# Twelve seven-product pairs in place of ten in the right half of an MLP's down-projection, at other places, and four additions moved from GpSimd to VectorE

## The chip, the cores and the metric

The kernel runs on one core of one Trainium2 chip. A core has TensorE (matrix products; the profile calls it PE, its weight loads PEld), VectorE (DVE), ScalarE (ACT), GpSimd (POOL) and SyncE (SP, which here only issues DMAs). The metric is the device time of one execution in microseconds, the median of the runs shown. The engines run side by side; each works through its own instructions in a fixed order and waits where an operand is not ready or a buffer is not free yet.

## The reference

Two decoder layers over 256 tokens of width 2048, in float32. Each layer has a mixer (attention and a short convolution, with projections in and out) and an MLP of width 8192; both add to x.

```python
for l in range(DEPTH):                       # DEPTH = 2
    h = _rmsnorm(x, attn_norm_g[l])
    proj = h @ w_in[l]                       # q, k, v, gates, convolution input
    ...
    x = x + jnp.concatenate([attn, conv], axis=-1) @ w_out[l]
    hm = _rmsnorm(x, mlp_norm_g[l]) @ w_up[l]               # (256, 2048) @ (2048, 8192)
    x = x + jnp.square(jax.nn.relu(hm)) @ w_down[l]         # (256, 8192) @ (8192, 2048)
```

The change is in the last line: the product with `w_down`, 8192 rows by 2048 columns a layer.

## The kernel before, in words

**Products.** Each float32 operand is split into a high and a low part that TensorE multiplies at its fast rate, and a product is three matmuls: high x high, high x low, low x high (`TERMS`). ScalarE makes a high part by copying (for a weight `whi`, L291), VectorE the low one by subtracting (`wlo`, L292).

**The MLP.** The 8192 hidden rows are worked off as 32 pairs of 128-row blocks, pair 0 to 31, in two passes.

- *First pass:* for each pair the up-projection (`up_part`, `upc` at L855), its squared ReLU (`square`), and, two pairs behind it (`LAG`), the left 1024 columns of the down-projection (`product`, `pr` at L903). At its end pairs 30 and 31 are left, whose left half has a loop of its own (L985, 48 matmuls in all, with weights `draw` and the activations f in two halves). The layer's sums for the left columns are then put together (`shared`, `onto`, and the loop ahead of `store`).
- *Second pass:* the right 1024 columns, pair 0 to 31, products named `rt`. The activations are read back from DRAM.

**Plain and seven-product pairs.** A 2x2 block product can be done with eight block products or with seven products of sums of blocks. A plain pair is eight products (24 matmuls, L1057; the last one at L1042). Its activations come ready split as `g`, a block for two pairs, loaded over GpSimd's queue. A seven-product pair is seven (21 matmuls, L903), but its operands have to be made. `quarters` makes the weights' from the pair's `raw`: b1 and b2 (ScalarE's b1h, b2h at L739, VectorE's b1l, b2l at L740); the sums t in three VectorE operations (L753, L756, L757); from t the parts t13h and t24h (ScalarE) and t13l and t24l (VectorE). `in_forms` makes the activations': h is read back by SyncE (`load_again`, h<-hid), four small VectorE operations (L889 to L892) add the sums, ScalarE copies f's high part (L894), and VectorE subtracts f's low part (L895). In the first pass every pair but the last two is a seven-product pair. In the second, those in `SEVEN` are.

**What sets the order.** TensorE's order is that of the code. For weights, `Weights.take` lets each be made three jobs ahead of its use (`AHEAD = 3`), in an order of jobs that the second pass lays out so: the plain pairs' half-pairs in sequence, and behind each of the four half-pairs ahead of a seven-product pair one of its four jobs (b1 and b2; t and t13; f; t24). Where the seven-product pair before stands only two pairs away, there is one plain pair between them, so two jobs go behind each of its two half-pairs:

```python
for i in SEVEN:
    before = [j for j in mine if j < where[i]][-4:]
    js = [where[i] + k for k in (1, 2, 0, 3)]
    if len(before) == 4 and SEVEN.index(i) and where[SEVEN[SEVEN.index(i) - 1]] > before[0]:
        before = [before[2], before[2], before[3], before[3]]
```

On the other engines a scheduler then fixes the order when the kernel is built. Buffers hold the work back further: three for the `raw` loads of a layer's MLP, three each for a weight's high and low part, two for b1, two for f, one each for b2, t13, t24, t and h. A buffer is written anew only once its readers are done, so a `whi` on ScalarE may wait for TensorE, and a load on SyncE for ScalarE and VectorE.

**Sums and the next norm.** `shared` (L964) forms e1 to e4 from the seven products' sums by `onto` (L961) and adds them to x. It is called once for the left half, ahead of the loop at L985, and once for the right half, behind the last seven-product pair. At the end of layer 0 the next layer's norm transposes x chunk by chunk (`norm.chunk`, `tpn` at L425) as background work between matmuls; `work.start(piece, wait)` puts it off by so many ticks, that is by groups of matmuls. At the end of layer 1 `store` writes the output over SyncE.

## Time and profile before

| | us |
|---|---|
| median of three runs | 2179.25 (2176.77 to 2180.44) |
| the profiled execution, its own time | 2180.75 |
| its span in the trace | 2178.7 |
| TensorE busy | 2151.5 (99%) |
| VectorE busy | 1690.1 (78%) |
| ScalarE busy | 1291.5 (59%) |
| GpSimd busy | 179.3 (8%) |

Three stages recur below. The end of the first pass (L985) lies at 910.57 to 928.21 in layer 0 and at 1990.66 to 2007.04 in layer 1; the second pass at 928.21 to 1098.05 and at 2007.04 to 2174.32. The rows of a timeline give the start in us, the duration, the engine, the line, and out<-in; `x4` behind a row is four instructions put together, and a bracket at the end is the time that the engine waited before it, with what ended the wait. A row of the view by windows gives a stretch, its length, then the busy time of TensorE, its weight loads, VectorE, ScalarE and GpSimd with the number of instructions, the granted clock of TensorE (1.00 is full speed), the busy share of the DMA engines and the GB/s. An engine's busy time says little here by itself: what counts is who is late for TensorE, and where.

### The profile page before, as it was taken

The numbers are of one execution on the slowest core, as the hardware profiler recorded it, in microseconds if no ns is written. First come the engines' busy times: TensorE is split into PE (matmuls) and PEld (weight loads), VectorE is DVE, ScalarE is ACT, GpSimd is POOL, SyncE is SP. The second block draws the span as 40 slices with busy tenths as digits, with TensorE's granted clock in tenths as the row PEclk, the third lists the DMA queues.
The fourth block names the chain that finished last, engine by engine and source line by source line (L and its number), as shares of the span: only waits on it lengthen the run. The fifth ranks groups of instructions, "written<-read, shape, count | busy, mean of one in ns | idle before, by whom it ended". The sixth has DMA issues, their size and how long they took to land.

```text
span 2178.7 us, 29219 instructions
## 1 busy us (share of the span) xinstructions
PE 2151.5 (99%) x11026; PEld 1824.4 (84%) x11026; DVE 1690.1 (78%) x2405; ACT 1291.5 (59%) x1748; POOL 179.3 (8%) x224
## 2 busy tenths in 40 slices
PE   8999999999999999999999999999999999999999
PEld 7888888888888888788878888888888888887887
DVE  5677655698888888898766776556988888888885
ACT  6456444566666666555554554455666666665553
POOL 3011100000000000200100211000000000002001
PEclk9999999999999999999999999999999999999999
DMA  7655766487777777877756566665777777768884
GB/s 254 175 156 174 220 185 189 149 254 219 230 228 218 228 223 230 262 263 266 268 147 182 155 191 206 185 187 180 237 235 224 222 223 226 230 215 275 289 288 137
DMA packets 286013, 469.71 MB, mean 216 GB/s; under 512 B 10579, under 2 KB 191397, under 8 KB 283056
## 3 DMA queue, kind: packets, MB, share of 16 engines
q1 hardware_dynamic: 267552, 412.13, 61.2%
q0 software_dynamic: 18272, 55.70, 7.5%
q8 instruction: 86, 1.41, 0.3%
q14 instruction: 55, 0.45, 0.1%
q10 hardware_dynamic: 48, 0.02, 0.0%
HBM read 437.37 MB, written 30.43 MB: 215 GB/s over the span
## 4 chain that ended last, share of the span: by engine, by line
PE 93%; DVE 2%; DMA 2%; issue 2%; ACT 1%; POOL 0%; ACTq 0%; POOLq 0%; DVEq 0%
PE upc L855 29%; PE pr L903 12%; PE rt L1057 10%; PE o L361 8%; PE rt L903 4%; PE gc L383 4%; PE ci L383 4%; PE gb L383 4%; PE v L361 4%; PE k L361 4%; PE q L361 3%; PE upw L855 1%; DMA uraw<-in_w_up_dram 1%; PE sc L525 1%; PE pr L985 1%
## 5 line engine op out<-in xcount | busy, mean ns | idle before, releaser
L292 DVE TENSOR_TENSOR wlo<-raw,whi 128x1024 fp32r<-128x1024 f32 (+1 forms) x346 | 426.9, 1235 | 272.8 <-ACT whi L291 268.1
L291 ACT ACTIVATE whi<-raw 128x1024 fp32r<-128x1024 f32 (+1 forms) x346 | 363.7, 1054 | 418.4 <-PE o L361 71.9
L855 PE MATMUL upc<-nT,uhi 128*128 128x512 f32 x1920 | 477.6, 391 | 0.0
L718 ACT ACTIVATE uhi<-uraw 128x1024 fp32r<-128x1024 f32 x256 | 271.2, 1060 | 290.2 <-PE upc L855 254.0
L855 PEld LDWEIGHTS upc<-nT,uhi 128*128 128x128 f32 x1920 | 352.7, 188 | 68.3
L719 DVE TENSOR_TENSOR ulo<-uraw,uhi 128x1024 fp32r<-128x1024 f32 x256 | 312.5, 1221 | 116.9 <-ACT uhi L718 110.8
L855 PEld LDWEIGHTS upc<-nT,ulo 128*128 128x128 f32 x1920 | 261.9, 190 | 18.7
L855 PE MATMUL upc<-nT,ulo 128*128 128x256 f32 x1920 | 267.7, 282 | 0.0
L1057 PE MATMUL rt<-whi,g 128*128 128x512 f32 x672 | 210.9, 389 | 0.0
L361 PE MATMUL o<-whi,cat 128*128 128x512 f32 x512 | 159.6, 390 | 0.0
L1057 PEld LDWEIGHTS rt<-whi,g 128*128 128x128 f32 x672 | 126.2, 188 | 26.1
L1057 PE MATMUL rt<-wlo,g 128*128 128x512 f32 x336 | 130.7, 389 | 0.0
L361 PEld LDWEIGHTS o<-whi,cat 128*128 128x128 f32 x512 | 96.2, 188 | 19.7
L895 DVE TENSOR_TENSOR f<-h,f 128x1024 fp32r<-128x1024 f32 (+1 forms) x84 | 102.3, 1218 | 0.0
L882 POOL DMA_DIRECT2D plain<-f x44 | 31.5, 715 | 832.7 <-DVE f L895 786.1
L361 PE MATMUL o<-wlo,cat 128*128 128x512 f32 x256 | 99.7, 389 | 0.0
L740 DVE TENSOR_TENSOR t13l<-t,t13h 128x1024 fp32r<-128x1024 f32 x80 | 97.9, 1223 | 1.9 <-ACT t13h L739 0.5
L740 DVE TENSOR_TENSOR t24l<-t,t24h 128x1024 fp32r<-128x1024 f32 x80 | 97.4, 1217 | 0.6 <-ACT t24h L739 0.3
L903 PE MATMUL pr<-t13h,f 128*128 128x512 f32 x240 | 93.8, 391 | 0.0
L894 ACT ACTIVATE f<-h 128x1024 fp32r<-128x1024 f32 (+1 forms) x84 | 86.1, 1025 | 4.7 <-DVE h L892 4.5
L361 PE MATMUL q<-whi,nT 128*128 128x512 f32 x256 | 85.4, 401 | 3.4 <-ACT whi L291 3.4
L739 ACT ACTIVATE t24h<-t 128x1024 fp32r<-128x1024 f32 x80 | 84.0, 1050 | 4.7 <-PE rt L903 3.0
(365 smaller groups left out, 3898.6 us busy)
## 6 DMA issues: line engine op xcount, KB each, us to landing
uraw<-in_w_up_dram SPq DMA_DIRECT2D x128, 1024.0 KB, 6.6
raw<-in_w_in_dram SPq DMA_DIRECT2D x191, 512.0 KB, 4.0
draw<-in_w_down_dram SPq DMA_DIRECT2D x64, 1024.0 KB, 5.2
raw<-in_w_down_dram SPq DMA_DIRECT2D x64, 1024.0 KB, 6.4
raw<-in_w_out_dram SPq DMA_DIRECT2D x64, 512.0 KB, 3.7
plain<-f POOLq DMA_DIRECT2D x44, 512.0 KB, 6.5
g<-plain POOLq DMA_DIRECT2D x22, 1024.0 KB, 6.3
hid<-h POOLq DMA_DIRECT2D x20, 256.0 KB, 6.2
```

Source lines behind the costliest of these rows:

```text
L291: a = nc.scalar.activation(hi[:, k], raw[:, k], AF.Copy)
L292: d = nc.vector.tensor_sub(lo[:, k], raw[:, k], hi[:, k].bitcast(F32))
L361: nc.tensor.matmul(acc[:, t], a.ap[:, pa, k % KG, t * P:(t + 1) * P], (hi, lo)[pw][:, j], start=(k == 0 and n == 0), stop=(k == nk - 1 and ...
L383: nc.tensor.matmul(acc[:, f, 0] if part else acc[:, f], wt[:, k % 4, fs], a.ap[:, 0, k % KG] if part else a.ap[:, :, k % KG], start=(part ...
L718: nc.scalar.activation(hi, src, AF.Copy)
L719: nc.vector.tensor_sub(lo, src, hi.bitcast(F32))
L740: keep(nc.vector.tensor_sub(lo, src, hi.bitcast(F32)))
L855: nc.tensor.matmul(acc[:, 0] if part else acc, wt[:, k], a.ap[:, 0, k % KG] if part else a.ap[:, :, k % KG], start=(part == 0 and kh == 0 ...
L894: nc.scalar.activation(f[:, 0, :n], h[:, :n], AF.Copy)
L895: nc.vector.tensor_sub(f[:, 1, :n], h[:, :n], f[:, 0, :n].bitcast(F32))
L903: nc.tensor.matmul(prods[n], f[:, pa, a], b[pw], start=(start and m == 0), stop=(stop and m == 2))
L1057: nc.tensor.matmul(prods[p], blocks[b][:, slot, pa, 2 * k + t], w[pw][:, n], start=(i == PLAIN[0] and k == 0 and m == 0), stop=False)
```

## The change

The pairs that use seven products in the second pass are twelve in place of ten, the first is pair 4 in place of 2, and from pair 7 to 25 they stand two apart in place of mostly three; the others are plain. The four additions of `shared` leave GpSimd: the function returns them, and VectorE does them, for the left half behind the `onto`s of the last two pairs, for the right half at once. The transposes of the next layer's last chunk are put off by 8 ticks in place of 2.

```diff
-SEVEN = (2, 5, 8, 11, 14, 16, 19, 22, 25, 27)
+SEVEN = (4, 7, 9, 11, 13, 15, 17, 19, 21, 23, 25, 28)
@@ shared
-                for dst, v in ((x11, e1), (x12, e4), (x21, e3), (x22, e3)):
-                    nc.gpsimd.tensor_tensor(dst, dst, v, op=ALU.add)
+                return [(x11, e1), (x12, e4), (x21, e3), (x22, e3)]
@@ ahead of the first pass's last two pairs
-            shared(*left)
+            sums = shared(*left)
@@ behind them
             for dst, (_, _, p) in zip(left, OWN):
                 onto(dst, prods[p], dst)
+            for dst, v in sums:
+                nc.vector.tensor_add(dst, dst, v)
@@ behind the last seven-product pair
-                        shared(*right)
+                        for dst, v in shared(*right):
+                            nc.vector.tensor_add(dst, dst, v)
@@ behind the last plain pair
-                                work.start(norm.chunk(2 + n, 2))
+                                work.start(norm.chunk(2 + n, 2 + 6 * n))
```

The diff leaves open what the scheduler makes of it. In the rows that follow, the numbers behind names tell buffers' contents apart, and lines of the changed kernel from 970 on are up to two off from those of before.

At the end of layer 1's first pass, VectorE has had these instructions from the last `onto`s of `shared` on (`f<-h,f 128x512` is the low part of pair 31's activations, `wlo<-draw` a weight of the last two pairs, `wlo<-raw` those of the second pass's first plain pairs):

```order
L961 SCALAR_TENSOR_TENSOR e_18283<-pr_13924,rowf_13666,e_18282 128x512
L874 TENSOR_TENSOR h<-h,ratiob 128x2x128
L961 SCALAR_TENSOR_TENSOR e_18285<-pr_13927,rowf_13666,e_18283 128x512
L961 SCALAR_TENSOR_TENSOR x_84<-pr_13927,rowf_13666,x_84 128x512
L961 SCALAR_TENSOR_TENSOR e_18284<-pr_13928,rowf_13666,e_18283 128x512
L740 TENSOR_TENSOR t24l<-t,t24h 128x1024
L292 TENSOR_TENSOR wlo<-draw,whi 128x1024
L895 TENSOR_TENSOR f<-h,f 128x512
L292 TENSOR_TENSOR wlo<-raw,whi 128x1024 x2
```

In the changed kernel the same place on VectorE reads:

```order
L961 SCALAR_TENSOR_TENSOR e_18319<-pr_13960,rowf_13702,e_18318 128x512
L874 TENSOR_TENSOR h<-h,ratiob 128x2x128
L961 SCALAR_TENSOR_TENSOR e_18321<-pr_13963,rowf_13702,e_18319 128x512
L961 SCALAR_TENSOR_TENSOR x_84<-pr_13963,rowf_13702,x_84 128x512
L961 SCALAR_TENSOR_TENSOR e_18320<-pr_13964,rowf_13702,e_18319 128x512
L895 TENSOR_TENSOR f<-h,f 128x512
L292 TENSOR_TENSOR wlo<-draw,whi 128x1024
L292 TENSOR_TENSOR wlo<-raw,whi 128x1024 x2
```

The t24l of the second pass's first seven-product pair has left this place, and f stands ahead of the wlo. The additions of the left half come further down, among the first weights of the second pass.

In the second pass, VectorE of the kernel before has these instructions up to the activations of pair 16, which stands two behind pair 14 (f_19018 is pair 16's, raw_18823 its weights, wlo_18861 and wlo_18895 belong to the plain pairs 15 and 17):

```order
L740 TENSOR_TENSOR b1l_18826<-raw_18823,b1h_18825 128x512
L756 TENSOR_TENSOR t_18872<-t_18872,raw_18823 128x512
L890 TENSOR_TENSOR h_18905<-h_18905 128x128
L292 TENSOR_TENSOR wlo_18861<-raw_18817,whi_18860 128x1024
L757 TENSOR_TENSOR t_18872<-raw_18823,t_18872 128x512
L892 TENSOR_TENSOR h_18905<-h_18905 128x128
L292 TENSOR_TENSOR wlo_18895<-raw_18892,whi_18894 128x1024
L740 TENSOR_TENSOR b2l_18830<-raw_18823,b2h_18829 128x1024
L740 TENSOR_TENSOR t13l_18875<-t_18872,t13h_18874 128x1024
L740 TENSOR_TENSOR t24l_18924<-t_18872,t24h_18923 128x1024
L895 TENSOR_TENSOR f_19018<-h_18905,f_19018 128x1024
```

Here f follows work for its own pair and one weight of the plain pair behind it. In the changed kernel VectorE has these up to the activations of pair 17 (f_19106; t_19158 and raw_19133 are pair 19's, raw_19115 is pair 18's, raw_19201 pair 20's):

```order
L740 TENSOR_TENSOR t13l_19073<-t_19070,t13h_19072 128x1024
L740 TENSOR_TENSOR t24l_19112<-t_19070,t24h_19111 128x1024
L889 TENSOR_TENSOR h_19021<-h_19021 128x128
L891 TENSOR_TENSOR h_19021<-h_19021 128x128
L753 TENSOR_TENSOR t_19158<-raw_19133 128x1024
L890 TENSOR_TENSOR h_19021<-h_19021 128x128
L292 TENSOR_TENSOR wlo_19173<-raw_19115,whi_19172 128x1024
L756 TENSOR_TENSOR t_19158<-t_19158,raw_19133 128x512
L892 TENSOR_TENSOR h_19021<-h_19021 128x128
L292 TENSOR_TENSOR wlo_19204<-raw_19201,whi_19203 128x1024
L757 TENSOR_TENSOR t_19158<-raw_19133,t_19158 128x512
L895 TENSOR_TENSOR f_19106<-h_19021,f_19106 128x1024
```

Now two operations on pair 19's sums and the first weight of pair 20 stand ahead of pair 17's f. On ScalarE the same holds: the last rows up to pair 17's f (f_19018 is pair 15's f) are

```order
L894 ACTIVATE f_19018<-h_18935 128x1024
L291 ACTIVATE whi_19117<-raw_19115 128x1024
L739 ACTIVATE b2h_19051<-raw_19045 128x1024
L739 ACTIVATE b1h_19135<-raw_19133 128x512
L739 ACTIVATE t13h_19072<-t_19070 128x1024
L739 ACTIVATE t24h_19111<-t_19070 128x1024
L291 ACTIVATE whi_19172<-raw_19115 128x1024
L291 ACTIVATE whi_19203<-raw_19201 128x1024
L894 ACTIVATE f_19106<-h_19021 128x1024
```

Both weights of pair 18 and the first of pair 20 are made between the f of pair 15 and the f of pair 17.

## Prediction

> **What bounds the kernel now.** I read the page first, then the stretches, the timelines of TensorE and VectorE, and the groups of the weight loads. The two stretches of some 17 us are the last two pairs of the first pass (layer 0, layer 1); the two long ones are the second pass.
>
> ```profile
> PE 2151.5 (99%) x11026; PEld 1824.4 (84%) x11026; DVE 1690.1 (78%) x2405; ACT 1291.5 (59%) x1748; POOL 179.3 (8%) x224
> ...
> 910.57:928.21 17.64, 14.04 (x49) 11.03 (x48) 12.96 (x13) 6.15 (x8) 8.20 (x5) 0.81 0.74 276
> 1990.66:2007.04 16.38, 12.79 (x49) 10.06 (x48) 12.77 (x13) 6.15 (x8) 8.20 (x5) 0.90 0.80 291
> 928.21:1098.05 169.84, 169.44 (x756) 140.09 (x754) 138.99 (x174) 95.14 (x111) 12.56 (x13) 1.00 0.75 259
> 2007.04:2174.32 167.28, 167.28 (x739) 138.33 (x737) 134.22 (x165) 87.00 (x89) 9.84 (x11) 1.00 0.71 244
> ```
>
> TensorE is the bound: in layer 1's second pass it is busy all the time, 167.28 us for 738 matmuls, 0.227 us each. So a plain pair (24 matmuls) lasts 5.45 us and a seven-product pair (21) 4.77. VectorE is busy for 134 of those 167 us, not far behind. TensorE does lose time at the end of the first pass: 48 matmuls take 17.64 and 16.38 us where 48 x 0.227 = 10.90, and the granted clock (last but two column) is 0.81 and 0.90.
>
> ```profile
> 1996.32 0.39 PE L985 MATMUL pr<-wlo,f 128*128 128x512 f32 x1
> 2000.30 0.73 PE L985 MATMUL pr<-whi,f 128*128 128x512 f32 x2 [3.59 <-DVE f L895]
> ...
> 1993.98 5.72 POOL L972 TENSOR_TENSOR x<-x,e 128x512 f32<-128x512 f32 x3 [1.03 <-DVE e L961]
> ...
> 1994.48 0.73 DVE L961 SCALAR_TENSOR_TENSOR e<-pr,rowf,e 128x512 f32<-128x512 f32 x1
> 1995.14 1.22 DVE L740 TENSOR_TENSOR t24l<-t,t24h 128x1024 fp32r<-128x1024 f32 x1
> 1996.29 2.30 DVE L292 TENSOR_TENSOR wlo<-draw,whi 128x1024 fp32r<-128x1024 f32 x1
> 1998.51 1.74 DVE L895 TENSOR_TENSOR f<-h,f 128x512 fp32r<-128x512 f32 x1
> 2000.17 1.21 DVE L292 TENSOR_TENSOR wlo<-raw,whi 128x1024 fp32r<-128x1024 f32 x1
> ...
> 2006.13 2.72 DVE L961 SCALAR_TENSOR_TENSOR x<-pr,rowf,x 128x512 f32<-128x512 f32 x4
> ```
>
> There TensorE waits 3.59 us for f of pair 31. Ahead of it VectorE has t24l of the first seven-product pair (1.15 us to the next start) and a wlo that takes 2.30 beside GpSimd's adds, as f takes 1.74; the next wlo, after the adds, takes 1.21.
>
> **The change, part by part.** *End of the first pass.* In the new order f(31) stands right behind the last e. Without t24l, wlo and GpSimd's adds it starts about when t24l starts now, 1995.14, and is done within 0.7 us, by 1995.9; TensorE wants its low part two matmuls past 1996.55. The next want, the last wlo, comes one job later, by 1997.1, for 1999.3. So both stretches shrink to 10.90: 6.74 + 5.48 = 12.2 us gained, half-clock time included.
>
> *Matmuls.* Two more seven-product pairs a layer, three matmuls fewer each: 12 x 0.227 = 2.7 us gained.
>
> *Transposes of the last chunk (wait 2 + 6n).* They stand behind 48 matmuls of the next layer's q in place of 12.
>
> ```profile
> 1101.68 0.60 PE L425 MATMUL tpn<-ident,x 128*128 128x128 f32 x4
> 1104.85 0.63 PE L425 MATMUL tpn<-ident,x 128*128 128x128 f32 x4 [2.57 <-DVE nT L256]
> ```
>
> Its 2.57 us wait goes, as 36 more matmuls (8.2 us) cover the release; 24 matmuls (5.4 us) remain before their result is asked for, against 0 now. Gain 2.6 us; bounds 0 and 2.6.
>
> *The second pass* decides. Rows of VectorE, ScalarE and TensorE around pairs 14 and 16, the one place of this trace before pair 25 where seven-product pairs stand two apart:
>
> ```profile
> 2072.20 1.22 DVE L895 TENSOR_TENSOR f<-h,f 128x1024 fp32r<-128x1024 f32 x1
> ...
> 2077.33 1.23 DVE L753 TENSOR_TENSOR t<-raw 128x1024 f32<-128x1024 f32 x1 [2.43 <-DMA raw<-in_w_down_dram]
> ...
> 2079.61 0.28 DVE L889 TENSOR_TENSOR h<-h 128x128 f32<-128x128 f32 x1
> 2079.81 0.28 DVE L891 TENSOR_TENSOR h<-h 128x128 f32<-128x128 f32 x1
> 2080.01 0.69 DVE L740 TENSOR_TENSOR b1l<-raw,b1h 128x512 fp32r<-128x512 f32 x1
> 2080.62 0.69 DVE L756 TENSOR_TENSOR t<-t,raw 128x512 f32<-128x512 f32 x1
> ...
> 2085.63 1.22 DVE L740 TENSOR_TENSOR t13l<-t,t13h 128x1024 fp32r<-128x1024 f32 x1
> 2086.77 1.22 DVE L740 TENSOR_TENSOR t24l<-t,t24h 128x1024 fp32r<-128x1024 f32 x1
> 2087.90 1.22 DVE L895 TENSOR_TENSOR f<-h,f 128x1024 fp32r<-128x1024 f32 x1
> ...
> 2098.51 1.22 DVE L895 TENSOR_TENSOR f<-h,f 128x1024 fp32r<-128x1024 f32 x1
> ...
> 2075.29 1.06 ACT L291 ACTIVATE whi<-raw 128x1024 fp32r<-128x1024 f32 x1 [1.65 <-PE rt L1057]
> ...
> 2085.44 1.06 ACT L739 ACTIVATE t24h<-t 128x1024 fp32r<-128x1024 f32 x1 [0.30 <-PE rt L903]
> 2086.41 1.04 ACT L894 ACTIVATE f<-h 128x1024 fp32r<-128x1024 f32 x1
> ...
> 2085.24 0.39 PE L1057 MATMUL rt<-whi,g 128*128 128x512 f32 x1
> ...
> 2090.68 0.39 PE L903 MATMUL rt<-b1h,f 128*128 128x512 f32 x1
> ...
> DMA to landing us min/median/max: 4.9/6.4/8.1
> ...
> raw<-in_w_down_dram SPq DMA_DIRECT2D x64, 1024.0 KB, 6.4
> ...
> g<-plain POOLq DMA_DIRECT2D x22, 1024.0 KB, 6.3
> hid<-h POOLq DMA_DIRECT2D x20, 256.0 KB, 6.2
> ```
>
> From these: VectorE starts an operation of 1024 elements every 1.14 us, of 512 every 0.60, of 128 every 0.20; ScalarE one of 1024 every 0.97 (done after 1.06). A tile that TensorE frees at a pair's end (2085.24) is written 0.20 later. f of pair 16 was ready at 2089.1, TensorE wanted it at 2090.68: 1.6 us to spare, where pair 14 (f at 2073.4, wanted at 2080.5) had 7.1. The last four rows are the time of a weight load in that pass and the sizes: 1 MB of weights a pair, half a MB of g for each of 44 plain pairs, a quarter for a seven-product pair.
>
> *The sums.* Four adds of 512 elements, 0.60 us each, join VectorE at both ends. At the left they lie ahead of the weights of pairs 1 and 2; priced in the walk below. At the right they lie beside pairs 29 to 31 (16 us, five VectorE weights): nothing. GpSimd only loses work. Layer 1's stores wait for the sums, and pair 3's load stands behind the stores on SyncE; its buffer comes free later still (7.9 us into the pass), so that costs nothing.
>
> VectorE's work for a seven-product pair is 4 x 1.14 (t, b2l, t13l, t24l) + 3 x 0.60 + 4 x 0.20 + 1.14 (f) = 8.30, for a plain pair 2.28. Two apart, that is 10.58 us while TensorE needs 4.77 + 5.45 = 10.22. The new pattern has nine such steps in a row, 7 to 25. By throughput alone 0.36 x 9 = 3 us would be lost at most, and the lead would swallow it. The queues' order does more.
>
> Pair 17: VectorE has wlo of pair 20's first half ahead of f(17), and ScalarE the whi of that half ahead of f(17). That whi reuses a buffer that TensorE frees at the end of pair 16. So even with all else early, f(17)'s low part is ready 0.20 + 1.06 + 0.04 (handing over) + 1.14 (wlo) + 0.60 (t) + 1.22 + 0.04 = 4.30 us after pair 16 ends, and TensorE, which wants it for its third matmul, 0.45 in, waits 3.85. Pair 15: t24l(15) and f(15) stand behind wlo of pair 16's second half, which needs a buffer freed 2.72 into pair 14: 2.72 + 0.20 + 1.06 + 0.04 + 1.14 + 1.14 + 1.22 + 0.04 = 7.56 after pair 13, wanted at 5.45 + 0.45 = 5.90: 1.66. These 5.5 us a layer are the floor.
>
> Loads add to it: a seven-product pair's load goes out when the plain pair three buffers back has been read. I walked the three queues row by row from the start of the pass (0.0), every row starting when its engine is free and what it waits for is done, with a load of 6.4. Where VectorE reaches wlo(2) only behind the sums and pair 4's t, b1l and b2l, at 10.7, it is done 0.9 after TensorE's want. Low part of f, ready/wanted: pair 7 27.3/38.8; 9 42.0/49.0; 11 57.3/59.2; 13 72.1/69.4; 15 84.9/82.3; 17 102.1/95.1 (pair 20's load goes out at 91.6, when b2l(17) is done, and lands at 98.0); 19 109.2/112.4; then t24l(21) 0.9 late, f(23) 0.7, f(25) 4.4. The steps of 15 us from 7 to 13 hold VectorE's waits for loads (the 2.43 above is one such). Sum 19.2 us a layer. With a load of 5.3, nearer the fastest: 0.9 at pair 2, 0.3 at 13, 1.9 at 15, 5.1 at 17, 2.7 at 25, sum 10.9. I take the middle, 15.0: the pass before mostly moves 4.25 MB in three pairs' 15.7 us, the new one 2.75 in two pairs' 10.2 and some 1.5 of waits, 14% less in a us, so loads should land a little faster than the median.
>
> *The clock.* What a wait of TensorE does to it:
>
> ```profile
> 413.96 1.30 PE L855 MATMUL up<-nT,uhi 128*128 128x512 f32 x3 [2.09 <-ACT ev L865]
> ...
> 411.00:414.39 3.39, 1.30 (x10) 1.05 (x9) 0.94 (x1) 1.54 (x2) 0.00 (x0) 1.00 1.01 367
> 414.39:417.81 3.42, 3.42 (x11) 2.77 (x10) 0.62 (x2) 0.32 (x1) 0.00 (x0) 0.50 0.23 80
> ```
>
> A 2.09 us wait that left TensorE busy for 1.30 of 3.39 us was followed by 3.42 us at half clock. The first pass's ends, waits of 3.6, cost beyond the wait (16.38 - 10.90 - 3.75) 1.7 and, in layer 0, 3.0. I take 2.3 a layer for pair 17 and 0.9 for the smaller waits: bounds 1.7 and 4.6.
>
> The Trainium skill ("TensorE: Matmul & The Clock Gate", HAM oscillation) puts the bar at idle gaps over about 3.4 us. The trace disagrees: 2.09 sufficed. By the page, the floor's waits, broken by two matmuls that need only f's high part, would cost no clock; the sum would be 2 x 0.9 lower.
>
> *Sum*, on the profiled execution's 2180.75: - 12.2 - 2.7 - 2.6 + 2 x (15.0 + 3.2) = + 18.9, so 2199.6; that execution was 1.5 over the median of the three runs, so 2198. The case's own range: 2 x (10.9 + 2.3) = 26.4 gives 2188, 2 x (19.2 + 4.6) = 47.6 gives 2209.
>
> **The rivals.** *Faster.* Loads land before they are asked for, only pairs 15 and 17 wait, and those waits don't halve the clock: 2180.75 - 17.5 + 2 x 5.5 - 1.5 = 2173. For it: pairs 16 to 19 now, where f follows f after 10.6 us (2087.90, 2098.51) with no load waited for. Against: 2072.20 to 2087.90, 15.7 us in the one step of the new kind. It decides below 6.5 us of waits a layer. The skill's rule on the clock above would speak for it.
>
> *No change.* The same floor with 2.3 us of half clock a layer: 2177.
>
> *Much slower.* Every step of two takes 15.7 as from 14 to 16: nine steps x (15.7 - 10.2) = 49.5, less the 11.4 that pair 7 has to spare, 38 a layer: 2238. The 10.6 step speaks against it.
>
> *The first pass's end doesn't shorten*, because another row takes f(31)'s place: 12.2 more than forecast, 2210. For it only that the new order is untested there; the walk has 1.1 to spare (1995.9 against 1997.0).
>
> **How the numbers follow.** Forecast 0.68, faster 0.13, no change 0.12, much slower 0.04, first pass unchanged 0.03. What a measurement can tell from no change is about 0.2%, 4.4 us. So faster 0.13, same 0.12, slower 0.75. The range 2176 to 2213 takes in the floor with the clock, the forecast with the slowest loads and the case without the first pass's gain; it leaves out 0.17.
>
> **What would show it.** Right: no wait of L985 on f, and both stretches near 11 us at clock 1.00; GpSimd without additions; in the second pass waits of TensorE for f at pairs 13, 15, 17 and 25, the longest at 17, a clock below 1.00 there, VectorE waiting for raw between; the second pass some 15 us longer than its 166. Wrong: TensorE without waits from pair 7 to 13 and at 25 (loads faster than 5.3), or waits at every pair. Most of all I could be wrong in how far the loads lag.

## The result and the profile after

The changed kernel takes 2195.58 us, the median of four runs (2192.67 to 2198.82), against 2179.32 before: a ratio of 1.0075 (95% interval 1.0063 to 1.0088), 16 us slower. The forecast was 2198.

The page of the changed kernel, its busy times and the chain that ended last; behind them the chain of the kernel before:

```profile
PE 2154.1 (98%) x11014; PEld 1821.4 (83%) x11014; DVE 1716.4 (78%) x2461; ACT 1299.7 (59%) x1760; POOL 148.7 (7%) x206
...
PE 82%; DVE 7%; DMA 7%; issue 2%; ACT 1%; POOL 0%; ACTq 0%; POOLq 0%; DVEq 0%; SPq 0%
```

```profile
PE 93%; DVE 2%; DMA 2%; issue 2%; ACT 1%; POOL 0%; ACTq 0%; POOLq 0%; DVEq 0%
```

TensorE has 12 matmuls fewer and is as busy as before in us, but 11 hundredths of the span have left it in the chain, to VectorE and the DMAs. The same stretches as those shown of before (end of the first pass in layer 0 and 1, second pass in layer 0 and 1):

```profile
906.54:917.42 10.88, 10.88 (x50) 9.01 (x48) 7.54 (x10) 5.18 (x7) 0.71 (x1) 1.00 0.96 343
1995.96:2006.84 10.88, 10.88 (x49) 9.01 (x48) 7.54 (x10) 5.18 (x7) 0.71 (x1) 1.00 0.98 346
917.41:1106.78 189.37, 175.52 (x749) 141.61 (x748) 161.61 (x210) 103.01 (x121) 4.99 (x8) 0.96 0.69 235
2006.84:2192.74 185.90, 172.36 (x733) 139.07 (x731) 157.75 (x201) 94.47 (x99) 3.19 (x6) 0.97 0.64 222
```

The account of the profiled execution, whose span grew by 18.3 (2178.7 to 2197.0):

| stage | before | after | change |
|---|---|---|---|
| layer 0 up to the end of its first pass | 910.57 | 906.54 | -4.0 |
| end of the first pass, layer 0 | 17.64 | 10.88 | -6.8 |
| second pass, layer 0 | 169.84 | 189.37 | +19.5 |
| layer 1 up to the end of its first pass | 892.61 | 889.18 | -3.4 |
| end of the first pass, layer 1 | 16.38 | 10.88 | -5.5 |
| second pass, layer 1, and what follows it | 171.66 | 190.16 | +18.5 |

So the first pass's ends gave 12.3 where 12.2 was forecast, and the second passes took 38. What TensorE waited for in them, first in layer 0, then in layer 1, by the view of waits (us in total, times, longest):

```profile
PE rt L903 <- ACT f L894: 9.7, 4, 6.5
PE rt L903 <- DVE f L895: 3.1, 4, 1.0
PE rt L1059 <- DVE wlo L292: 0.7, 1, 0.7
PE rt L1044 <- DVE x L961: 0.3, 1, 0.3
...
PE rt L903 <- ACT f L894: 8.7, 4, 5.1
PE rt L903 <- DVE f L895: 4.2, 4, 2.0
PE rt L1059 <- DVE wlo L292: 0.7, 1, 0.7
```

These are 13.8 and 13.5 us a layer. From the starts of the pairs' first matmuls, the time that a pair and the start of the next one lost against 5.44 (plain) or 4.76 (seven products), half clock included:

| lost at | layer 0 | layer 1 | forecast, without the clock (loads of 5.3 to 6.4 us) |
|---|---|---|---|
| pair 2 | 1.0 | 1.0 | 0.9 |
| pairs 12 and 13 | 2.9 | 2.9 | 0.3 to 2.7 |
| pairs 14 and 15 | 2.0 | 1.9 | 1.9 to 2.6 |
| pairs 16 and 17 | 10.9 | 8.3 | 5.1 to 7.0 |
| pairs 20 to 23 | 0 | 0 | 0 to 1.6 |
| pairs 24 and 25 | 4.1 | 5.7 | 2.7 to 4.4 |

Over the whole pass that is 20.9 us in layer 0 and 20.0 in layer 1. In layer 0 the 2.5 us are left out that its last four pairs lose before the change too, beside the next layer's transposes; all losses of a second pass below are counted so.

The longest wait is that of pair 17. VectorE and ScalarE ahead of it, in layer 0, and TensorE:

```profile
1006.12 1.22 DVE L740 TENSOR_TENSOR b2l<-raw,b2h 128x1024 fp32r<-128x1024 f32 x1
1010.38 0.69 DVE L740 TENSOR_TENSOR b1l<-raw,b1h 128x512 fp32r<-128x512 f32 x1 [3.04 <-ACT b1h L739]
...
1015.15 0.28 DVE L890 TENSOR_TENSOR h<-h 128x128 f32<-128x128 f32 x1
1015.35 1.22 DVE L292 TENSOR_TENSOR wlo<-raw,whi 128x1024 fp32r<-128x1024 f32 x1
1016.48 0.68 DVE L756 TENSOR_TENSOR t<-t,raw 128x512 f32<-128x512 f32 x1
1017.09 0.28 DVE L892 TENSOR_TENSOR h<-h 128x128 f32<-128x128 f32 x1
...
1009.71 0.63 ACT L739 ACTIVATE b1h<-raw 128x512 fp32r<-128x512 f32 x1 [4.73 <-DMA raw<-in_w_down_dram]
...
1017.40 1.06 ACT L894 ACTIVATE f<-h 128x1024 fp32r<-128x1024 f32 x1 [2.10 <-DVE h L892]
...
1018.51 0.79 PE L903 MATMUL rt<-b1h,f 128*128 128x512 f32 x1 [6.53 <-ACT f L894]
```

ScalarE waits 4.73 us for the load of pair 19, VectorE's b1l of pair 19 waits for ScalarE, and the last of pair 17's four sums (L892) stands behind all that and behind a weight of pair 18. From 1010.38 on VectorE works almost without a break up to f. The load of pair 19 was slow itself. It went out at 999.63, when its buffer came free, and a 1 MB load of g went out 0.4 us behind it. Both took 10.1 us, where the median weight load of the second passes takes 5.4 (in layer 1, where the wait is 5.1, they took 8.6 and 9.6). The DMA issues between 999.0 and 1000.1:

```profile
raw<-in_w_down_dram SPq DMA_DIRECT2D x1, 1024.0 KB, 10.1
g<-plain POOLq DMA_DIRECT2D x1, 1024.0 KB, 10.1
```

After the wait the clock is halved (three stretches of TensorE, granted clock in the last column but two):

```profile
1018.50:1021.90 3.40, 2.82 (x6) 1.82 (x7) 1.74 (x2) 0.12 (x1) 0.00 (x0) 0.50 0.85 319
1021.90:1025.30 3.40, 3.40 (x10) 2.63 (x9) 1.39 (x4) 0.51 (x1) 0.00 (x0) 0.50 0.12 43
1025.30:1028.70 3.40, 3.40 (x15) 2.77 (x14) 2.22 (x3) 3.02 (x4) 0.00 (x0) 0.87 0.00 0
```

### The profile page after: what moved, and what is told of

Its sections match the earlier page's. It is cut to its first block, busy times and chain, and to the rows that moved or that the text cites. A ratio compares the mean times of both kernels' runs of the same rounds, so it can differ in the third digit from the quotient of the medians.

```text
span 2197.0 us, 29226 instructions
## 1 busy us (share of the span) xinstructions
PE 2154.1 (98%) x11014; PEld 1821.4 (83%) x11014; DVE 1716.4 (78%) x2461; ACT 1299.7 (59%) x1760; POOL 148.7 (7%) x206
## 4 chain that ended last, share of the span: by engine, by line
PE 82%; DVE 7%; DMA 7%; issue 2%; ACT 1%; POOL 0%; ACTq 0%; POOLq 0%; DVEq 0%; SPq 0%
PE upc L855 29%; PE pr L903 13%; PE o L361 8%; PE gc L383 4%; PE ci L383 4%; PE gb L383 4%; PE v L361 4%; PE k L361 4%; DMA raw<-in_w_down_dram 4%; PE rt L1059 3%; PE q L361 3%; DVE wlo L292 2%; PE rt L903 1%; DMA uraw<-in_w_up_dram 1%; PE upw L855 1%
## 5 line engine op out<-in xcount | busy, mean ns | idle before, releaser
L292 DVE TENSOR_TENSOR wlo<-raw,whi 128x1024 fp32r<-128x1024 f32 (+1 forms) x338 | 414.9, 1229 | 257.8 <-ACT whi L291 256.5
L291 ACT ACTIVATE whi<-raw 128x1024 fp32r<-128x1024 f32 (+1 forms) x338 | 354.9, 1053 | 371.5 <-PE o L361 73.6
L1059 PE MATMUL rt<-whi,g 128*128 128x512 f32 x608 | 191.8, 389 | 0.0
L1059 PEld LDWEIGHTS rt<-whi,g 128*128 128x128 f32 x608 | 114.1, 188 | 23.8
L1059 PE MATMUL rt<-wlo,g 128*128 128x512 f32 x304 | 118.5, 390 | 1.4 <-DVE wlo L292 1.4
L740 DVE TENSOR_TENSOR t13l<-t,t13h 128x1024 fp32r<-128x1024 f32 x84 | 102.6, 1222 | 2.0 <-ACT t13h L739 1.0
L740 DVE TENSOR_TENSOR t24l<-t,t24h 128x1024 fp32r<-128x1024 f32 x84 | 102.2, 1217 | 1.9 <-ACT t24h L739 1.7
L739 ACT ACTIVATE t13h<-t 128x1024 fp32r<-128x1024 f32 x84 | 88.3, 1051 | 4.1 <-PE rt L903 3.7
```

The source lines that it names most:

```text
L291: a = nc.scalar.activation(hi[:, k], raw[:, k], AF.Copy)
L292: d = nc.vector.tensor_sub(lo[:, k], raw[:, k], hi[:, k].bitcast(F32))
L739: keep(nc.scalar.activation(hi, src, AF.Copy))
L740: keep(nc.vector.tensor_sub(lo, src, hi.bitcast(F32)))
L1059: nc.tensor.matmul(prods[p], blocks[b][:, slot, pa, 2 * k + t], w[pw][:, n], start=(i == PLAIN[0] and k == 0 and m == 0), stop=False)
```

## The experiments

The theory behind the forecast: in the second pass the queues' order makes a floor of 5.5 us a layer (pairs 15 and 17), and late loads make the rest. The rivals: VectorE's work for two pairs (10.58 us against TensorE's 10.22), or the additions and not the places of the pairs. All ratios are against the kernel before, run beside each kernel.

| kernel | median, us | ratio (95% interval) |
|---|---|---|
| sums | 2177.76 | 0.9998 (0.9989 to 1.0007) |
| seven | 2190.70 | 1.0059 (1.0046 to 1.0071) |
| chunk_only | 2176.41 | 0.9984 (0.9975 to 0.9992) |
| ten_from_4 | 2163.22 | 0.9930 (0.9916 to 0.9944) |
| ten_later_sums | 2169.41 | 0.9956 (0.9944 to 0.9968) |
| f_kept | 2183.53 | 1.0027 (1.0017 to 1.0036) |
| two_h | 2182.37 | 1.0012 (0.9994 to 1.0029) |
| five_buffers | 2185.76 | 1.0040 (1.0025 to 1.0056) |
| less_vector | 2163.42 | 0.9929 (0.9917 to 0.9941) |
| fixed_order | 2246.43 | 1.0299 (1.0285 to 1.0313) |
| fixed_order_less | 2220.44 | 1.0178 (1.0164 to 1.0192) |
| f_stored | 2161.62 | 0.9909 (0.9894 to 0.9924) |

### The three parts alone

**sums**: the old ten pairs and the old wait, VectorE's additions.

```diff
-SEVEN = (4, 7, 9, 11, 13, 15, 17, 19, 21, 23, 25, 28)
+SEVEN = (2, 5, 8, 11, 14, 16, 19, 22, 25, 27)
...
-                                work.start(norm.chunk(2 + n, 2 + 6 * n))
+                                work.start(norm.chunk(2 + n, 2))
```

> The old ten pairs and the old wait of 2 for the last chunk; only the four additions of each half are VectorE's. In VectorE's order t24l of pair 2 and a wlo still stand ahead of f(31). Theory (f(31) is late because of what stands ahead of it, and GpSimd's additions slow that): without them t24l, wlo and f take 1.14 + 1.14 + 0.64 from 1995.14, f is ready at 1998.1, wanted at 1997.0, so TensorE waits about 1.1 in place of 3.6 at both ends, the half clock there may go or stay: 5 to 9.7 us gained, 2170 to 2175. Rival (the place of the first seven-product pair alone makes the gain): 2179, TensorE still waits 3.6.

Measured: no change, so the theory's 2170 to 2175 is missed; its mechanism held. These are waits of TensorE in the view of waits, both layers together. The row with `pr` is that of the first pass's end, the two with `rt` are those of the second pass's first seven-product pair, which is pair 2 here:

```profile
PE rt L903 <- DVE f L895: 2.1, 2, 1.1
PE pr L984 <- DVE f L895: 2.0, 2, 1.0
PE rt L903 <- ACT f L894: 1.8, 2, 0.9
```

The wait at the end of the first pass shrank from 3.6 to 1.0 us, as the theory had it (1.1), and the stretch kept its full clock: from its first matmul to the second pass's it lasts 12.2 us in both layers. But the additions, now ahead of the weights of pairs 1 and 2, cost 2.5 us a layer there (6.49 + 6.26 against 5.44 + 4.76 in layer 0), a wait that the forecast of this run had left out. So of 9.6 us gained at the two ends (from 17.64 and 16.38), 5.0 go again just behind them. The profiled executions do differ by the other 4.6 (spans of 2178.7 and 2174.2), the medians do not. Part of the reason is on record. In the profiled execution of chunk_only (below), whose instructions up to there are those of before, the wait of layer 0's end is 3.6 us as well, but the clock stays at 1.00 and the end lasts 14.8 us in place of 17.6:

```profile
908.27:923.08 14.81, 11.22 (x50) 8.93 (x48) 12.16 (x12) 6.16 (x8) 8.21 (x5) 1.00 0.87 325
```

So the half clock at that place comes in some executions and not in others, and in a median the ends are worth less than in the profiled execution of before. How much less isn't shown.

**seven**: the new pairs alone.

```diff
-SEVEN = (2, 5, 8, 11, 14, 16, 19, 22, 25, 27)
+SEVEN = (4, 7, 9, 11, 13, 15, 17, 19, 21, 23, 25, 28)
```

> Only the new twelve pairs; GpSimd adds and the chunk's wait of 2 stay. f(31) stands right behind the last e, but beside GpSimd's additions it may take 1.74: ready at 1996.9, wanted at 1997.0. Theory: both ends of the first pass are near 11 us all the same, the 2.6 us wait of the chunk stays, the second pass loses as in the changed kernel, less up to 0.9 a layer at pair 2: 2196 to 2199. Rival (the additions on VectorE make the gain at the end of the first pass): 7 to 12 us more, 2203 to 2208.

Measured 2190.7, 5 us below the theory's range and further from the rival's. TensorE waits for nothing at L985, and both ends take 10.9 us, with GpSimd still adding. So it is the place of f(31), behind the last e, that mends the first pass's end, and not the additions' engine. The second pass loses 15.2 and 15.0 us a layer (against its matmuls' time) where the changed kernel loses 20.9 and 20.0, and at other pairs: mostly 19 to 21 and 6, in place of 15 to 17 and 25. The scheduler laid its queues out otherwise.

**chunk_only**: the longer wait of the last chunk alone.

```diff
-                                work.start(norm.chunk(2 + n, 2))
+                                work.start(norm.chunk(2 + n, 2 + 6 * n))
```

> The kernel before with the last chunk's wait of 8 ticks in place of 2. Theory: the wait of 2.57 us for the chunk's transposes goes, nothing comes in its place: 2.6 us below before. Rival (q waits for the chunk's nT later instead): 0 to 1 us below.

Measured 0.16% less, 3.5 us with an interval of 1.7 to 5.4, and no wait for nT is left, here or in the changed kernel: the theory. The three parts alone add up to +12.9 - 0.4 - 3.5 = 9.0, the whole is 16.3; the parts do not add, since each gives the scheduler other queues.

### Fewer steps of two

**ten_from_4**: all three parts, but ten pairs.

```diff
-SEVEN = (4, 7, 9, 11, 13, 15, 17, 19, 21, 23, 25, 28)
+SEVEN = (4, 7, 10, 13, 16, 18, 21, 24, 26, 28)
```

> As the changed kernel, but ten pairs, (4, 7, 10, 13, 16, 18, 21, 24, 26, 28): mostly three apart, three steps of two (16 to 18, 24 to 26, 26 to 28), never more than two of them in a row. Theory (the loss is made by many steps of two in a row, which eat the lead of 11 us; the gains at the first pass's end and at the chunk don't hang on them): 2179.3 - 12.2 - 2.6 = 2164.5, at most 3 us lost about pair 2 and pair 28: 2162 to 2168. Rival (each step of two costs 1.7 to 3.9 us by the queues' order): three steps in two layers, 2174 to 2185.

Measured 2163.2, as the theory said, 15 us below before. In its second passes TensorE waits only at pair 2, but for 0.3 us at layer 0's last pair (0.4 before):

```profile
PE rt L1059 <- DVE wlo L292: 1.4, 2, 0.7
```

So the gains do not hang on the twelve pairs, and one or two steps of two in a row (16 to 18, 24 to 26 to 28) cost nothing.

**ten_later_sums**: ten_from_4 with the additions of the left half behind pair 7 of the second pass, kept there. Layer 1's stores of that half move with them.

```diff
-            for dst, v in sums:
-                nc.vector.tensor_add(dst, dst, v)
...
             for i in range(NP):
+                if i == 8:
+                    for dst, v in sums:
+                        tc.keep_in_program_order(nc.vector.tensor_add(dst, dst, v))
...
```

> As the kernel with ten pairs from 4 on, but the four additions of the left half are put behind pair 7 of the second pass (and the last layer's stores of that half with them), where VectorE has time. Theory (the additions ahead of wlo(2) make the 1.05 us wait at pair 2): the wait goes in both layers, 2 us: 2160.5 to 2162. Rival (other work ahead of wlo(2) makes it, or the later stores delay a load): 2163 or more.

Measured 2169.4: worse by 6. The loss at pair 2 shrank from 1.0 to 0.3 us, but pair 6 lost 4.4 and 2.8. With the additions gone the scheduler put other work in their place (pair 4's t13l ahead of pair 2's second wlo, among others), and loads went out bunched: in layer 0 three weight loads, issued within 3.5 us, took 9.2, 12.1 and 14.6 us. Ahead of pair 6's weights ScalarE waited 4.5 and 2.9 us for their load, and VectorE for ScalarE. So a queue that looks roomier need not be faster, once the scheduler has laid it out anew.

### Order, loads or work

**f_kept**: the two instructions of f keep the program's order in the second pass.

```diff
-                    f = in_forms(again[i], True)
+                    f = in_forms(again[i], True, late)
...
-                nc.scalar.activation(f[:, 0, :n], h[:, :n], AF.Copy)
-                nc.vector.tensor_sub(f[:, 1, :n], h[:, :n], f[:, 0, :n].bitcast(F32))
+                keep(nc.scalar.activation(f[:, 0, :n], h[:, :n], AF.Copy))
+                keep(nc.vector.tensor_sub(f[:, 1, :n], h[:, :n], f[:, 0, :n].bitcast(F32)))
```

> As the changed kernel, but the two instructions that make f of a seven-product pair in the second pass keep their place in the program's order, so that on VectorE f(15) and f(17) stand right behind their own pair's t24l and no weight of pair 18's second half or of pair 20 stands ahead of f(17). The work and the loads are the same. Theory (queue order makes the floor at 15 and 17, late loads the rest): the waits at pair 17 shrink from 10.9 and 8.3 us a layer to what the loads make, 2 to 5 us a layer, half-clock stretches mostly gone: 2173 to 2185. Rival (steps of two need more of VectorE and the loads than the time of the two pairs, so a wait that is taken away at 17 comes back at 19 to 25): 2192 to 2198.

Measured 2183.5, 12 below the changed kernel: within the theory's range, at its upper end. Pairs 15 and 17 wait for nothing, but pairs 11 to 13 now lose 4.4 and 8.3 us, and 19 to 25 some 2.4 and 6.7: of what was taken away at 17 a good part came back elsewhere. In all, the second passes lose 8.8 and 17.1 us. The order decides where, and how much, but it is not the whole.

**two_h**: h is read back into two buffers, a pair earlier.

```diff
-                again[i] = fpool.tile([P, 8, P], F32, tag="h", name="h", bufs=1)
+                again[i] = dpool.tile([P, 2, 2 * CH], F32, tag="draw", name="h2")[:, 0].rearrange(
+                    "p (a c) -> p a c", c=P)
...
-                    later = SEVEN.index(i) + 1
+                    later = SEVEN.index(i) + 2
...
+            load_again(SEVEN[1])
```

> As the changed kernel, but the activations h of seven-product pairs are read back into two buffers (the idle draw) in place of one, a pair earlier. VectorE's order then has each f ahead of its own pair's t24l, f(15) and f(17) too. Weight loads still have three buffers. Theory (order makes the floor, loads the rest): the long waits at pair 17 go, waits of 2 to 4 us come at other pairs where loads are late: 2180 to 2188. Rival (the one buffer of h, which is loaded only when the f before is done, was the whole cause): no waits for f at all, 2162 to 2168.

Measured 2182.4, but spread over 2170 to 2190. f is never late; t24l is, which now stands behind the next pair's f:

```profile
PE rt L904 <- DVE t24l L740: 11.5, 8, 4.0
PE rt L904 <- ACT t24h L739: 3.2, 4, 1.5
```

The theory's time is met, and of the rival the half that no f is late, but not its time: the one buffer of h was not the whole cause. VectorE, put in another order, is late with something else, and the second passes lose 6.2 and 20.1 us.

**five_buffers**: the weight loads of the second pass over five buffers.

```diff
+                own = col and i % 5 in (0, 2, 4)
-                raw = (upool.tile([P, 2, 2 * CH], F32, tag="uraw", name="raw") if col else
+                raw = (upool.tile([P, 2, 2 * CH], F32, tag="uraw", name="raw") if own else
                        dpool.tile([P, 2, 2 * CH], F32, tag="draw", name="draw"))
```

> As the changed kernel, but the second pass's weight loads take turns over five buffers in place of three: two of five go to the buffers draw that the first pass used and that lie idle here. VectorE's work is the same; f(15) and f(17) still stand behind weights of later pairs on VectorE. Theory (late loads make about two thirds of the loss, the queues' order a floor of 5.5 us a layer): a load is asked for some 10 us earlier, the waits at 13 and 25 go, and those at 15 to 17 shrink to the floor and its half clock: 2176 to 2184. Rival (VectorE's work, 10.58 us for two pairs that TensorE does in 10.22, and its order make it): 2190 to 2196.

Measured 2185.8: 10 below the changed kernel, 2 short of the theory's range and 4 short of the rival's. Waits of 8.3 and 4.6 us a layer stay, at pairs 14 to 25, and the second passes lose 11.5 and 8.9 us where the changed kernel loses 20.9 and 20.0. So earlier loads take away half of that loss. The time shows less of it, since the first pass's ends grow at once from 10.9 to 13.5 and 14.8 us: VectorE's order is another there too, and f(31) is late again, by 2.0 and 1.65 us.

**less_vector**: 1.1 us less VectorE work in each seven-product pair, as two of the four sums are left out.

```diff
-                    keep(nc.vector.tensor_add(t[:, 2], t[:, 1], raw[:, 0, 0]))
-                    keep(nc.vector.tensor_sub(t[:, 3], raw[:, 1, 0], t[:, 2]))
+                    n = 1 if col else CH
+                    keep(nc.vector.tensor_add(t[:, 2, :n], t[:, 1, :n], raw[:, 0, 0, :n]))
+                    keep(nc.vector.tensor_sub(t[:, 3, :n], raw[:, 1, 0, :n], t[:, 2, :n]))
...
-                    h, lw = parts(forms["t"][:, 2:4], "t24", 1)
+                    t = forms["t"]
+                    h, lw = parts(t[:, 2:4] if not col else t[:, 0:2], "t24", 1)
```

> As the changed kernel, but in the second pass the two sums t2 and t4 are left out of the work (L756 and L757 add one column of 512, and the parts t24 are made from t1 and t3), so those products are not the reference's. VectorE saves about 1.1 us a seven-product pair: 9.5 us for two pairs in place of 10.58, against TensorE's 10.22. Its order changes with it: every f stands right behind the t24l of the pair before. Theory (loads three buffers deep are late whatever VectorE does): 4 to 10 us of waits a layer stay, 2178 to 2190. Rival (VectorE's throughput makes the loss): nearly all waits go, 2160 to 2166.

Measured 2163.4: the rival, and 32 us below the changed kernel. From pair 9 to 25 of layer 1 TensorE never waits; at pairs 2, 3 and 6 its second passes still lose 2.6 and 3.1 us. That stretch here, and in the changed kernel:

```profile
2039.00:2120.60 81.60, 81.60 (x361) 67.57 (x360) 77.60 (x114) 54.54 (x58) 1.59 (x3) 1.00 0.82 275
```

```profile
2055.50:2152.00 96.50, 85.65 (x362) 68.33 (x360) 84.20 (x111) 52.04 (x57) 1.59 (x3) 0.96 0.64 218
```

TensorE needs 81.6 us for these eight steps. VectorE has 84.2 us of work in them in the changed kernel, so more than there is time, and 77.6 here, so less. The weights are still loaded over three buffers. Since the order changed too (each f stands behind the t24l of the pair before), two more kernels hold it fixed.

**fixed_order**: every instruction of the second pass on weights, sums and activations keeps the program's order.

```diff
-                keep = late if i == 0 and col == 0 else lambda ins: None
+                keep = late if (i == 0 and col == 0) or col else lambda ins: None
...
-                if first:
+                if first or hold:
                     late(a)
                     late(d)
...
```

> As the changed kernel, but in the second pass every instruction on weights, sums and activations keeps the program's order, so that VectorE's order is the same for each step of two: t24l of the pair before, a wlo, b1l, b2l, t, t13l, t, t, a wlo, f. Full work. Theory (VectorE's work for two pairs is over TensorE's time for them, so that its waits for loads are never made up): 2180 to 2195. Rival (only the scheduler's order with later pairs' weights ahead of f is to blame): 2162 to 2172, as no f stands behind a weight of a later pair here.

**fixed_order_less** is that kernel with the edit of less_vector; the rows of VectorE, ScalarE and SyncE stand in the same order in both.

> The kernel with the fixed order, and L756 and L757 of the second pass add one column of 512, t24 is made from t1 and t3 (so these products are not the reference's). The order on VectorE, ScalarE and SyncE is the same, row by row, as with full work. Theory (VectorE's work decides): 15 to 25 us below the kernel with the fixed order, 2160 to 2172. Rival (the order of the kernel with less VectorE work, not the saved time, took its waits away): within 5 us of the kernel with the fixed order.

Measured 2246.4 and 2220.4. The first refutes both expectations: this order is far worse than the scheduler's, as at each plain pair TensorE waits for the second wlo, which stands behind the seven-product pair's t13l, t and t. The view of waits, first with full work, then with less:

```profile
PE rt L1060 <- DVE wlo L292: 52.3, 30, 2.3
```

```profile
PE rt L1062 <- DVE wlo L292: 27.9, 26, 1.2
```

The second lies 26 us below the first, just over the theory's 15 to 25, and far above its 2160 to 2172. So the pair of them does tell what the saved time alone is worth in that order: 26 us for 24 pairs, 1.1 each, just what VectorE saves. The two shortened sums stand right ahead of the wlo that is late here. So where VectorE is late in this order, each us of its work is paid in full; the order says at which instruction. That the same holds in the scheduler's order isn't shown by these two.

**f_stored**: the first pass stores the split f in place of h, and the second only loads it.

```diff
-            hid = {i: dram.tile([P, 4 * P], F32, name=f"hid{l}_{i}") for i in SEVEN}
+            hid = {i: dram.tile([P, 2, 8, P], F32R, name=f"hid{l}_{i}") for i in SEVEN}
...
-                again[i] = fpool.tile([P, 8, P], F32, tag="h", name="h", bufs=1)
-                nc.sync.dma_start(again[i][:, :4].rearrange("p a c -> p (a c)"), hid[i])
+                again[i] = fpool.tile([P, 2, 8, P], F32R, tag="f", name="f2")
+                nc.gpsimd.dma_start(again[i], hid[i])
...
-                    f = in_forms(again[i], True)
...
+                    return again[i]
...
-                if i in hid:
-                    nc.gpsimd.dma_start(hid[i], u)
                 f = in_forms(h, i < NP - LAG)
-                if i not in hid:
+                if i in hid:
+                    nc.gpsimd.dma_start(hid[i], f)
+                else:
```

> As the changed kernel, but the first pass stores the split f of seven-product pairs (1 MB) in place of h (a quarter), and the second loads it over GpSimd's queue; the four small sums, ScalarE's and VectorE's part of f go: VectorE 10.58 - 1.94 = 8.64 us for two pairs, the loads 3.5 MB in place of 2.75 in 10.2 us, which is 360 GB/s. The second pass with less VectorE work moved 275 GB/s at a DMA share of 0.82, that is 335 at full share. Theory (VectorE's work is the bound before, the DMAs become it here): waits for loads of up to 6 us a layer, 2162 to 2172. Rival (the load buffers make the loss): 2180 or more.

Measured 2161.6, 0.9% below before, a little better than the theory's range. Of the kernels that compute the whole product it is the best with ten_from_4; those two can't be told apart. The same stretch as above, the DMA issues in it, and the weight loads of the changed kernel's stretch:

```profile
2039.10:2120.70 81.60, 81.60 (x361) 67.59 (x360) 71.36 (x74) 44.88 (x49) 5.83 (x11) 1.00 0.96 357
...
raw<-in_w_down_dram SPq DMA_DIRECT2D x17, 1024.0 KB, 7.8
f<-hid POOLq DMA_DIRECT2D x8, 1024.0 KB, 7.9
```

```profile
raw<-in_w_down_dram SPq DMA_DIRECT2D x16, 1024.0 KB, 5.4
```

Here a weight load takes 7.8 us in place of 5.4, the DMAs are 96% busy, there are three buffers as before, and TensorE waits for nothing in this stretch. What was taken away is 1.94 us of VectorE's work for a pair, the h that is read back, and 0.97 us of ScalarE's.

## Why the prediction was right, and where it was not

- *First pass's end: right.* 12.3 us against 12.2, the clock at 1.00, no wait for f(31). There is luck in the closeness: both numbers lean on one execution of before, and chunk_only's had ends of 14.8 and 16.3 us, 2.9 less in sum, at the same waits. Its reasons stood side by side (t24l and wlo ahead of f, GpSimd's additions); seven and sums part them: the place of f suffices alone, the additions alone bring 3.6 down to 1.0.
- *Twelve matmuls and the chunk: right.* The 2.57 us wait is gone, and chunk_only has 3.5 (1.7 to 5.4) against 2.6.
- *The additions: right in the place (1.0 us at pair 2 against 0.9)*; sums shows that they cost more, 2.5, where pair 2 is a seven-product pair.
- *The waits of the second pass: right in place and size.* 13.8 and 13.5 us a layer against 15.0, at pairs 2, 13, 15, 17 and 25, longest at 17; those of 21 and 23 did not come. The walk took one load time throughout, 6.4 or 5.3 us; the load behind the longest wait took 10.1 and 8.6.
- *The clock: too small, and a small term was missing.* The passes lost 20.9 and 20.0 us against their matmuls' time, so 7.1 and 6.5 a layer beyond the waits, where 3.2 was taken with an upper bound of 4.6. Not all of this is the clock: at pair 13 of layer 0, where the clock stays at 1.00, two waits of 2.4 us together cost 2.9. With some 0.3 us for each of nine waits, about 2 us a layer are of that kind, and no term had them. The rest is the clock. With TensorE at work it stood at half for 7.7 us behind pair 17 in layer 0, 5.3 in layer 1, and for 3.4 us at pair 25 in both. At half, matmuls start 0.43 us apart in place of 0.23, so these cost an estimated 3.6, 2.5 and 1.6 us: 5.2 and 4.1 a layer. So both terms were mis-sized, "2.3 a layer for pair 17" (3.6 and 2.5) and "0.9 for the smaller waits" (1.6). Behind pair 25's two waits of just under 1 us the clock was halved in part of the third and fourth of these stretches (layer 0):

```profile
1059.00:1062.40 3.40, 3.40 (x17) 2.82 (x16) 3.40 (x7) 2.36 (x3) 0.00 (x0) 1.00 0.89 305
1062.40:1065.80 3.40, 2.01 (x8) 1.03 (x6) 3.40 (x4) 2.53 (x3) 0.00 (x0) 1.00 0.73 239
1065.80:1069.20 3.40, 2.86 (x8) 2.30 (x9) 3.40 (x5) 1.13 (x2) 0.00 (x0) 0.70 0.40 151
1069.20:1072.60 3.40, 3.40 (x13) 2.70 (x12) 3.40 (x7) 2.05 (x2) 0.00 (x0) 0.80 0.84 267
```

  There TensorE was busy for 2.01 of 3.40 us ahead of the slower stretch. That alone does not decide: at pair 13, waits of 1.65 and 0.71 us left it busy for 1.36 of 3.40 us, and the clock stayed at 1.00, in the stretch behind this one too:

```profile
986.00:989.40 3.40, 1.36 (x5) 0.48 (x3) 2.78 (x3) 3.40 (x5) 0.00 (x0) 1.00 0.45 186
```

  The Trainium skill ("TensorE: Matmul & The Clock Gate", HAM oscillation), which puts the bar at idle gaps over some 3.4 us, is not borne out here, as the prediction had said. What decides whether a wait costs clock, these runs do not show.
- *The cause of the waits: right in the mechanism, wrong in its weights.* The prediction took 5.5 us a layer from the queues' order, the rest from late loads, and of VectorE's excess it said that "by throughput alone 0.36 x 9 = 3 us would be lost at most, and the lead would swallow it". That sentence is the step that failed. The speed of the loads was no bound by itself: f_stored loads more, each load takes longer, and from pair 9 to 25 TensorE waits for nothing. Their median is shorter than before (5.4 us for 6.4). Loads are late here because they are asked for late, and at the longest wait because two of 1 MB were asked for together as well. In the changed kernel's layer 1 (2030 to 2170), SyncE's queue waited for VectorE to free a buffer:

```profile
SPq L726 <- DVE wlo L292: 53.5, 12, 7.4
SPq L805 <- DVE f L895: 24.3, 10, 5.3
SPq L726 <- DVE b2l L740: 17.5, 6, 5.0
SPq L726 <- DVE t L757: 13.9, 3, 6.0
```

  This view does not show the cause by itself, as SyncE waits for VectorE in kernels without loss too (from pair 9 to 25 of layer 1: before, 72.8 of 83.6 us; less_vector, 72.0 of 81.6; the changed kernel, 85.6 of 96.5). The account that fits the runs is a ring: a late VectorE makes late loads, and these make it wait, with no slack to make the wait up. Of the 40.9 us that the two second passes lose, another order leaves 25.9 (f_kept) or 26.3 (two_h), and five buffers leave 20.4. With 1.1 or 1.94 us less work a pair 5.6 and 3.1 are left, none of it from pair 9 on, and the times fall by 32 and 34 us. The walk came out near, since it carried VectorE's rows along with the loads; what it said about the cause was wrong.
- *4.0 us in layer 0 ahead of the first pass's end* were in no term. The kernel of chunk_only, whose instructions up to there are those of before, was 2.3 us ahead of before's profiled execution at the same matmul. An estimated 1.6 of it is the 3.4 us of half clock at 414.39 that the prediction shows, which neither chunk_only's nor the changed kernel's execution has. So most of it is the spread between executions, and the agreement of the sums to 3 us has some luck in it: the second passes took 4 us more than forecast, and this gave it back.

What stays open is whether VectorE's work decides by its sum over TensorE's time (84.2 over 81.6) or as the length of the chain from a freed buffer to the next wanted tile. less_vector and f_stored shorten both, and both change the order; in the fixed order it is the chain. What part of the loss is due to loads that ran at the same time isn't settled either; no run moved the loads of g alone.

## What to carry to other kernels

When a second engine's work comes up to the bounding engine's time (here 84.2 us against 81.6), its in-order waits can no longer be made up, and it is not enough to price the excess per step: 3 us a layer were priced, and 13.5 were waited for. Of a late load, ask who freed its buffer and what was loaded beside it. Before more products are saved on TensorE, the operands' making should leave the pass, as storing f did, or the saving be spaced so that single tight steps have roomy ones behind them.

## What the runs showed of the hardware that was not expected

- Two waits of TensorE of just under 1 us, 1.7 us apart, were followed by a stretch at a granted clock of 0.70; the prediction's shortest wait with that effect was 2.09. Waits of 1.65 and 0.71 us, 1.5 us apart, left it at 1.00.
- With 357 GB/s and a DMA share of 0.96 over 82 us, a 1 MB load took 7.8 us in place of 5.4, and TensorE kept its full clock and pace. Two 1 MB loads issued 0.4 us apart took 10.1 us each, and three weight loads issued within 3.5 us up to 14.6.
- A single wait of 1.0 us left the clock of the first pass's end at 1.00 (sums). Waits of 3.6 us brought it to 0.81 and 0.90 in one execution of before, and in layer 0 of chunk_only's one left it at 1.00.
- A wait of TensorE cost some 0.3 us more than the idle time in the profile, at full clock too (2.9 lost for 2.4 at pair 13).
